# A hybrid decoder layer on one core: second score product on 128 rows, vector work moved from POOL to DVE at the feed forward, adaLN products in pairs

## The chip, the cores and the metric

The program runs on one core of a Trainium2 chip. The metric is the device time of one execution in microseconds (us). The engines are named as in the profile: PE (TensorE, matmuls; PEld is its weight load), DVE (VectorE), ACT (ScalarE), POOL (GpSimd) and SP (SyncE, which here only issues DMAs).

## The reference, cut to what matters

One layer runs over 1024 prompt rows and 32 sample rows (1056 rows in all), D_MODEL 1024, 8 heads of 64, everything in float32:

```python
mod = silu(c) @ w_ada + b_ada
sh1, sc1, g1, sh2, sc2, g2 = split(mod, 6)
h = rmsnorm(x) * (1 + sc1) + sh1
z = h @ w_in + b_in
s = (q . k) / 8 + C_q - C_k
o = softmax(causal(s)) @ v
m = sigmoid(z_a) * (o @ w_pa) + sigmoid(z_b) * (conv_branch(z) @ w_pb + b_pb)
x = x + g1 * (m @ w_o)
h2 = rmsnorm(x) * (1 + sc2) + sh2
f_gate, f_up = split(h2 @ w_ffn_in, 2)
x = x + g2 * ((silu(f_gate) * f_up) @ w_ffn_out)
```

The conditioning vector c gives six adaLN vectors of 1024; the sixth, g2, is used only in the last line. Outputs are the normalised x and the new keys, values, forget values and convolution states.

## The kernel before, in words

The kernel keeps activations transposed (channels on the 128 partitions, rows in the free dimension). Every float32 operand of a large product is split into a high and a low float32r part, and a product is the sum of three matmuls: high by high, high by low, low by high. ACT makes the high part by a copy, DVE or POOL the low part by a subtraction.

A tile framework takes the program as written and chooses the order of each engine's instructions itself, with a planner that simulates the program with its own costs. What it may not change is the data flow and what goes through `in_order` (keep_in_program_order). `tc.high_priority(offset)` lets instructions be planned as if they had been written that much earlier. On the chip each engine, and each engine's DMA queue (SP's, ACT's, POOL's), then works strictly in the planned order, and an instruction whose semaphore is not there holds up all that stand behind it. Tiles of one tag share `bufs` buffers, so a load waits until the buffer's last reader is done.

The stages in order of time: start, first adaLN vectors and first projections (0 to 125 us); values, queries, keys, decode attention, GLU and convolution (125 to 430); prompt attention with gate projections (`gate`) and adaLN products as filler (430 to 672); remaining gates, branch products and `w_o` (672 to 895); entry of the feed forward (895 to 990); feed forward's first product (990 to 1400) and its second (1400 to 1671).

The places that the change touches:

- `ada(i, ...)`, L153: one adaLN vector. For each of 8 tiles k of `w_ada` (128x1024, 512 KB) SP loads a tile `wa` (L158), then four matmuls of 32 columns of the array run on it (L162). For vectors 2 to 5 the tile lies in the tag `wr` of pool `wp`, three buffers that are also those of the gate weights (L306) and of the feed forward's raw weights (L1117). Vectors 2 to 5 are called after the gates 6, 5, 4 and 3 in the loop over gates behind the attention; the planner moves them into the attention as filler.
- `softmax_rows(h, i, ...)`, L803: the scores of head h, block i of 128 rows, in stretches of 512 keys: L813 multiplies the tile `q` (128 rows: high and low part of the query) by `k` (the key's high part twice), L815 adds the mask on the diagonal, L816 multiplies the query's high part by the key's low part on the 64 rows `sl` only. There are 12 such stretches for each of 8 heads, 96 in all. DVE then takes the minimum (L818), ACT the exponential (L824), and `weighted` transposes (L871) and multiplies with the values (L883, L884).
- `load_head(h)`, L834: SP loads q (L846), k (L847), the 64 rows of kl (L848, 256 KB), ck (L849) and vh (L850).
- `half_factors`, L991: the factors of a Strassen-like product for half of the rows (528 columns as two times 264); L1030 and L1033 are subtractions on POOL, `split_u` (L1018) takes the low part on DVE or POOL (L1020).
- `split_w`, L302, its low part at L315; with `w_o` and the last third of the rows every second tile goes to POOL.
- `pair_weights(t, eng)`, L1128: seven weight factors from two raw tiles, with four add or subtract instructions of 128x512 (L1134, L1136, L1137, L1139) on DVE, or on POOL where a weight serves one half of the rows (t = 1, 2, 3, both times). `split` (L1120) makes the high part on ACT (L1124) and the low part on DVE (L1125); L1167 multiplies.

Of the kernel before, what the change touches and what calls it, by code (L numbers as in the profile page):

```python
# [9 lines left out]
F32 = mybir.dt.float32  # L10
# [35 lines left out]
KS = 2  # L46
NHR = 8
HF = 2
DV = (0,)
UW = KL + NP + DB * (KL + DT)  # L50


# [35 lines left out]
def hybrid_step(ctx, tc, xT, cT, vec, bvf, con, stT, ptab, ptabr, kcT, vc, lfc, w_ada, w_in, w_vfa, w_vfb,  # L88
# [64 lines left out]
    def ada(i, pl, tag, bufs, psum):  # L153

        ps = psum()
        for k in range(KD):
            w = pl.tile([P, KD, P], F32, name="wa", tag=tag, bufs=bufs).rearrange("p a b -> p (a b)")
            d = sp.dma_start(w, w_ada[k * P:(k + 1) * P, i * 1024:(i + 1) * 1024])  # L158
            if i < 2:
                in_order(d)  # L160
            for g in range(4):
                pe.matmul(ps[32 * g:32 * g + 32, :256], cTt[:, k, :], w[:, g * 256:(g + 1) * 256],  # L162
                          start=(k == 0), stop=(k == KD - 1))
        with tc.high_priority() if i < 2 else nullcontext():
            s = ev(wp, "gev", 4)
            d = act.copy(s[:, :256], ps[:, :256])
            if i == 1:
                in_order(d)
            pt = psum()
            for q in range(2):  # L170
                pe.transpose(pt[:, q * P:(q + 1) * P], s[:, q * P:(q + 1) * P], ident)
            src = pt[:, :256].rearrange("p (q g r) -> p g q r", q=2, g=4)[:, :, :, 0:9]
            b = V[:, V_ADA + i * 8:V_ADA + i * 8 + 8].rearrange("p (g q) -> p g q", g=4)
            dve.tensor_tensor(mod[:, i * 8:(i + 1) * 8, :].rearrange("p (g q) r -> p g q r", g=4),
                              src, b.unsqueeze(3).broadcast_to([P, 4, 2, 9]), OP.add)
            if i == 1:
                gains(0, V_RMS1, 8)
# [624 lines left out]

    def softmax_rows(h, i, t, ck, q, k, kl):  # L803

        sl = slice(64 * (h % 2), 64 * (h % 2) + 64)
        n = P * (i + 1)
        m = sm.tile([P, 4], F32, name="mx", tag="mx", bufs=6)
        prev = 3e38
        qb = slice(i * P, (i + 1) * P)
        for nm, s0 in enumerate(range(0, n, 512)):  # L810
            w = min(512, n - s0)
            ps = ps_s()
            pe.matmul(ps[:, :w], q[:, qb], k[:, s0:s0 + w], start=True, stop=False)  # L813
            if s0 + w == n:
                pe.matmul(ps[:, w - P:w], identr, maskr, start=False, stop=False)  # L815
            pe.matmul(ps[:, :w], q[sl, qb], kl[sl, s0:s0 + w], start=False, stop=True)  # L816

            dve.tensor_tensor_reduce(out=t[:, s0:s0 + w], in0=ps[:, :w], in1=ck[:, s0:s0 + w], scale=1.0, scalar=prev,  # L818
                                     op0=OP.add, op1=OP.min, accum_out=m[:, nm:nm + 1])
            prev = m[:, nm:nm + 1]  # L820
        cq = Cq[:, i, h:h + 1]
        st = sm.tile([P, 4], F32, name="st", tag="st", bufs=6)
        dve.scalar_tensor_tensor(st[:, 1:2], prev, cq, cq, op0=OP.subtract, op1=OP.add)
        act.activation(t[:, :n], t[:, :n], AF.Exp, bias=st[:, 1:2], scale=-1.0, accum_out=st[:, 2:3])  # L824
        dve.reciprocal(st[:, 3:4], st[:, 2:3])
        if h % 2 and i % 2:
            act.activation(t[:, :n], t[:, :n], AF.Copy, scale=st[:, 3:4])
        else:
            dve.tensor_scalar(t[:, :n], t[:, :n], st[:, 3:4], None, OP.mult)
        return t  # L830
# [3 lines left out]
    def load_head(h):  # L834

        p, h2 = divmod(h, 2)
        qd, kd = qkD[p]
        sl = slice(64 * h2, 64 * h2 + 64)

        def head_tile(name, dt=F32R):  # L840
            return atl.tile([P, NP], dt, name=name, tag=f"{name}{h2}", bufs=1)

        q, k, kl = head_tile("q2"), head_tile("k2"), head_tile("kl")
        ck, vh = head_tile("ck", F32), head_tile("vh").rearrange("p (b n) -> p b n", n=P)
        for r in range(2):
            sp.dma_start(q[64 * r:64 * r + 64, :].bitcast(F32), qd[r ^ h2][sl, :])  # L846
            sp.dma_start(k[64 * r:64 * r + 64, :].bitcast(F32), kd[0][sl, :])  # L847
        sp.dma_start(kl[sl, :].bitcast(F32), kd[1][sl, :])  # L848
        sp.dma_start(ck, cD[h:h + 1, :].broadcast_to([P, NP]))  # L849
        sp.dma_start(vh.bitcast(F32), vD[p][:, :, h2, :])  # L850
        heads[h] = (q, k, kl, ck, vh)
# [59 lines left out]
        weighted(*x)  # L911
    for i in (9, 8, 6, 5, 4, 3, 2, 1, 0):
        gate(i, pool, sp)
        if 3 <= i < 7:
            ada(8 - i, wp, "wr", 3, ps_mm)
    gains(1, V_RMS2, 32)
    atl.release()
# [75 lines left out]
    def half_factors(q, new):  # L993
# [21 lines left out]
                act.copy(u[:, :, n:], msf[:, 4 * i:4 * i + 4, :])  # L1015
            return u

        def split_u(b, k, u, eng=dve):  # L1018
            act.copy(b[0][:, k, :], u[:, k, :])
            eng.tensor_tensor(b[1][:, k, :], u[:, k, :], b[0][:, k, :].bitcast(F32), OP.subtract)  # L1020

        ks = [slice(KS * k, KS * k + KS) for k in range(4 // KS)]
        u11, u21, u12, u22 = [modulated(i, half) for half in range(2) for i in range(2)]
# [3 lines left out]
        for k in ks:  # L1027
            split_u(b21, k, u21)
        for k in ks:
            pool.tensor_tensor(u11[:, k, :], u12[:, k, :], u11[:, k, :], OP.subtract)  # L1030
            split_u(t1, k, u11)
        for k in ks:
            pool.tensor_tensor(u12[:, k, :], u22[:, k, :], u12[:, k, :], OP.subtract)  # L1033
            split_u(b22, k, u22, pool)
            dve.tensor_tensor(u22[:, k, :], u22[:, k, :], u11[:, k, :], OP.subtract)
            split_u(t2, k, u22)
        for k in ks:
            split_u(t3, k, u12, pool)
        for k in ks:
            dve.tensor_tensor(u21[:, k, :], u21[:, k, :], u22[:, k, :], OP.subtract)  # L1040
            split_u(t4, k, u21)
# [26 lines left out]
    for c in range(3):  # L1068
        o = CW3 * c
        s = sm.tile([P, 400], F32, name="s1", tag="ssum", bufs=2)  # L1070
        for j in range(KD):

            where = () if c == 0 and j < 2 else (lt2, ("wh3", "wl3"), 3)
            w = split_ahead(w_o[j], KD, pool if c == 2 and j % 2 else dve, *where)
            xr = ev(lt2, "xr", 3)
            for ch, (co, cn) in enumerate(CH):
                lo, hi = max(o, co), min(o + CW3, co + cn)
# [47 lines left out]
        dve.tensor_tensor(w[:, 1, :n], raw, w[:, 0, :n].bitcast(F32), OP.subtract)  # L1125
        return w

    def pair_weights(t, eng):  # L1128

        g, u = [raw_tile(w_fi[r * HT + t], KD * P) for r in range(2)]  # L1130
        a11, a12, a21, a22 = g[:, :512], g[:, 512:], u[:, :512], u[:, 512:]
        ws = [split(a11), split(a12)]
        s1 = ev(fb or uq, "s1", 2 if fb else 1, (P, 512))
        eng.tensor_tensor(s1, a21, a22, OP.add)  # L1134
        ws.append(split(s1))
        eng.tensor_tensor(a21, a11, a21, OP.subtract)  # L1136
        eng.tensor_tensor(a11, s1, a11, OP.subtract)  # L1137
        ws.append(split(a11))
        eng.tensor_tensor(a12, a12, a11, OP.subtract)  # L1139
        ws.append(split(a12))  # L1140
        ws.append(split(a21))
        ws.append(split(a22))
        return ws
# [7 lines left out]
    def hidden(t, halves):  # L1151


        with tc.high_priority(offset=OW if len(halves) == 2 else ON):
            w = pair_weights(t, dve if len(halves) == 2 or t in DV else pool)
        for q in halves:
            hidden_half(t, q, w)

# [40 lines left out]

    for t in range(NF):  # L1200
        hidden(t, (0,))
        if t == HF:
            B.append(half_factors(1, lambda: by_four(
                [x[:, i, :] for x in [lt.tile([P, 4, T], F32R, name="c", tag=tag, bufs=1) for tag in ("XA", "XB")] for i in range(4)] +
# [194 lines left out]
```

## Time and profile before

| | us |
|---|---|
| three runs, median (lowest to highest) | 1672.14 (1669.34 to 1674.14) |
| the profiled execution | 1673.01 |
| its span, first to last instruction | 1671.2 |
| PE busy in the span | 1600.6 |
| DVE busy | 1074.1 |
| ACT busy | 702.6 |
| POOL busy | 251.9 |

The busy time of PE is that of modelled, pipelined matmuls: a matmul's recorded duration includes its latency, so what it costs in a full queue is read from the distance between two starts. The granted clock is 1.00 at 2.4 GHz and 0.50 at 1.2 GHz.

### The profile page before, as it was taken

How to read it: one execution, taken by the hardware profiler on the slowest of the kernel's cores; microseconds unless marked ns; L12 is line 12 of the kernel's file. 1: busy time of each engine (PE TensorE's matmuls, PEld its weight loads, DVE VectorE, ACT ScalarE, POOL GpSimd, SP SyncE). 2: the span in 40 equal slices, each digit the busy share in tenths (PEclk: the TensorE clock that was granted, in tenths of full speed). 3: DMA queues.
4: the chain of work that ended last, by engine and by line, in shares of the span. 5: the costliest groups of instructions: out<-in, count | busy, mean ns of one | idle time of the engine just before them, and what ended most of it. 6: DMA issues, size and time to landing. Idle time of an engine off the chain costs nothing.

```text
span 1671.2 us, 29144 instructions
## 1 busy us (share of the span) xinstructions
PE 1600.6 (96%) x10988; PEld 1486.8 (89%) x10988; DVE 1074.1 (64%) x2119; ACT 702.6 (42%) x1395; POOL 251.9 (15%) x185
## 2 busy tenths in 40 slices
PE   6999999999999999999999789999999999999997
PEld 4999978788867777989998779999999999999997
DVE  6943389999787757234678995555555587324654
ACT  4552212122476555434554554333333365324442
POOL 2121113332220001125305430000000030000000
PEclk9999999999999979999999899999999999999998
DMA  9186576877486654354674322222222246424552
GB/s 363 62 285 185 159 226 176 249 234 224 150 247 211 185 166 145 114 187 123 211 219 156 102 85 101 77 77 77 77 82 83 80 155 214 157 87 146 172 184 84
DMA packets 143087, 263.93 MB, mean 158 GB/s; under 512 B 26810, under 2 KB 84794, under 8 KB 142306
## 3 DMA queue, kind: packets, MB, share of 16 engines
q1 hardware_dynamic: 104466, 211.46, 40.6%
q10 hardware_dynamic: 36384, 43.01, 7.4%
q0 software_dynamic: 2096, 7.60, 1.5%
q8 instruction: 86, 1.41, 0.4%
q14 instruction: 55, 0.45, 0.1%
HBM read 208.54 MB, written 53.48 MB: 157 GB/s over the span
## 4 chain that ended last, share of the span: by engine, by line
PE 70%; DVE 14%; DMA 7%; issue 3%; ACT 3%; SPq 2%; POOL 1%; ACTq 0%; DVEq 0%; POOLq 0%
PE mm L1167 23%; PE mm L1268 15%; DVE acc L525 7%; PE mm L326 6%; PE mm L324 6%; PE mm L325 6%; PE ptr L871 2%; PE pss L816 2%; DMA wa<-w_ada 1%; DMA gev<-gD 1%; PE ppv L884 1%; DVE wc L1125 1%; PE mm L162 1%; PE ppv L883 1%; PE pss L813 1%
## 5 line engine op out<-in xcount | busy, mean ns | idle before, releaser
L324 PE MATMUL mm<-ah,wh 128*128 128x384 f32 (+2 forms) x768 | 254.2, 332 | 7.4 <-ACT ah L288 3.6
L1268 PE MATMUL mm<-f,wo 128*128 128x352 f32 x1584 | 256.7, 323 | 0.0
L1268 PEld LDWEIGHTS mm<-f,wo 128*128 128x128 f32 x1584 | 254.7, 188 | 0.0
L326 PE MATMUL mm<-ah,wl 128*128 128x384 f32 (+2 forms) x768 | 253.0, 331 | 1.5 <-POOL wl L315 1.5
L325 PE MATMUL mm<-al,wh 128*128 128x384 f32 (+2 forms) x768 | 254.2, 331 | 0.0
L1167 PE MATMUL mm<-b,wc 128*128 128x264 f32 x1680 | 229.6, 288 | 10.3 <-ACT gev L1172 6.9
L1167 PE MATMUL mm<-c,wc 128*128 128x264 f32 x1776 | 235.5, 286 | 3.3 <-DVE gev L1189 3.3
L1167 PEld LDWEIGHTS mm<-c,wc 128*128 128x128 f32 x1776 | 225.2, 189 | 3.7 <-DVE gev L1189 3.7
L1167 PEld LDWEIGHTS mm<-b,wc 128*128 128x128 f32 x1680 | 217.0, 191 | 11.7 <-ACT gev L1172 7.3
L315 POOL TENSOR_TENSOR wl<-wr,wh 128x1024 fp32r<-128x1024 f32 (+1 forms) x48 | 122.1, 2547 | 440.3 <-ACT wh L312 417.3
L525 DVE SCALAR_TENSOR_TENSOR acc<-u,vec,acc 128x1024 f32<-128x1024 f32 x120 | 174.1, 1472 | 1.2
L324 PEld LDWEIGHTS mm<-ah,wh 128*128 128x128 f32 x768 | 146.5, 191 | 19.2 <-issue 7.9
L325 PEld LDWEIGHTS mm<-al,wh 128*128 128x128 f32 x768 | 146.6, 191 | 12.2 <-issue 11.7
L326 PEld LDWEIGHTS mm<-ah,wl 128*128 128x128 f32 x768 | 146.4, 191 | 7.6 <-issue 4.9
L1219 DVE TENSOR_TENSOR wo<-wr,wo 128x512 fp32r<-128x512 f32 x108 | 69.7, 647 | 129.7 <-ACT wo L1218 129.1
L1124 ACT CAST wc<-wr 128x512 fp32r<-128x512 f32 x144 | 88.0, 620 | 131.2 <-PE mm L1167 123.9
L1125 DVE TENSOR_TENSOR wc<-wr,wc 128x512 fp32r<-128x512 f32 x144 | 108.6, 760 | 37.1 <-ACT wc L1124 36.0
L1218 ACT CAST wo<-wr 128x512 fp32r<-128x512 f32 x108 | 63.2, 585 | 150.3 <-PE mm L1268 145.4
L312 ACT CAST wh<-wr 128x1024 fp32r<-128x1024 f32 (+1 forms) x72 | 68.1, 951 | 91.3 <-PE mm L325 71.9
L1134 POOL TENSOR_TENSOR s<-wr 128x512 f32<-128x512 f32 x6 | 13.1, 2188 | 400.6 <-DMA wr<-w_fi 387.1
L326 PE MATMUL mm<-yh,wl 128*128 128x352 f32 x192 | 61.9, 325 | 1.2 <-POOL wl L315 1.2
L324 PE MATMUL mm<-b,wh 128*128 128x352 f32 x192 | 62.1, 323 | 0.8 <-ACT wh L312 0.8
(299 smaller groups left out, 2731.6 us busy)
## 6 DMA issues: line engine op xcount, KB each, us to landing
wr<-w_fi SPq DMA_DIRECT2D x52, 512.0 KB
wa<-w_ada SPq DMA_DIRECT2D x48, 512.0 KB
wr<-w_fo SPq DMA_DIRECT2D x36, 512.0 KB
kt<-kcT SPq DMA_DIRECT2D x64, 256.0 KB
vt<-vc SPq DMA_DIRECT2D x64, 256.0 KB
wr<-w_o SPq DMA_DIRECT2D x24, 512.0 KB
hD<-h ACTq DMA_DIRECT2D x44, 264.0 KB
wr<-w_in SPq DMA_DIRECT2D x18, 512.0 KB
```

The source lines that it names most:

```text
L312: d = act.copy(wh[:, r, :], raw[:, r, :])
L315: eng.tensor_tensor(wl[:, r, :], raw[:, r, :], wh[:, r, :].bitcast(F32), OP.subtract)
L324: pe.matmul(ps[:, :n], wh[:, k, :], xh, start=(k == 0), stop=False)
L325: pe.matmul(ps[:, :n], wh[:, k, :], xl, start=False, stop=False)
L326: pe.matmul(ps[:, :n], wl[:, k, :], xh, start=False, stop=(k == nk - 1))
L525: dve.scalar_tensor_tensor(a[:, :NP], u[:, j:j + NP], wv[:, j:j + 1], a[:, :NP], op0=OP.mult, op1=OP.add)
L1124: act.copy(w[:, 0, :n], raw)
L1125: dve.tensor_tensor(w[:, 1, :n], raw, w[:, 0, :n].bitcast(F32), OP.subtract)
L1167: pe.matmul(ps[:, :HS], w[i][:, r, k * P:(k + 1) * P], x[s][:, k, :], start=(new and k == 0 and j == 0), stop=(k == 3 and j == 2), skip_gr ...
L1218: act.copy(x[:, 0, :], raw)
L1219: dve.tensor_tensor(x[:, 1, :], raw, x[:, 0, :].bitcast(F32), OP.subtract)
L1268: pe.matmul(ps[e][:, :n], w[r][:, k * P:(k + 1) * P], f[x], start=(k0 + k + i == 0), stop=(k0 + k == HT - 1 and i == 2))
```

## The change

`ada`: for the vectors 2 to 5 the tiles are loaded two at a time; the product of the second tile is issued first, and that of the first tile behind it is kept in program order. The vector 5 (the sixth) is no longer computed behind gate 3 but inside the feed forward, behind the first weight tile. In `load_head` all of q, k and kl are loaded on 128 rows, and L816 uses all of them (so it adds the product of the low parts). POOL's subtractions and additions in `half_factors`, `split_u`, `pair_weights` and the split of `w_o` go to DVE.

```diff
@@ ada
-        for k in range(KD):
+        def load(k):
             w = pl.tile([P, KD, P], F32, name="wa", tag=tag, bufs=bufs).rearrange("p a b -> p (a b)")
             d = sp.dma_start(w, w_ada[k * P:(k + 1) * P, i * 1024:(i + 1) * 1024])
             if i < 2:
                 in_order(d)
+            return w
+
+        def product(k, w, first, last, pinned=False):
             for g in range(4):
-                pe.matmul(ps[32 * g:32 * g + 32, :256], cTt[:, k, :], w[:, g * 256:(g + 1) * 256],
-                          start=(k == 0), stop=(k == KD - 1))
+                mm = pe.matmul(ps[32 * g:32 * g + 32, :256], cTt[:, k, :], w[:, g * 256:(g + 1) * 256],
+                               start=first, stop=last)
+                if pinned:
+                    in_order(mm)
+
+        if i < 2:
+            for k in range(KD):
+                product(k, load(k), k == 0, k == KD - 1)
+        else:
+            for k in range(0, KD, 2):
+                w0, w1 = load(k), load(k + 1)
+                product(k + 1, w1, k == 0, False)
+                product(k, w0, False, k == KD - 2, True)
@@ softmax_rows
-            pe.matmul(ps[:, :w], q[sl, qb], kl[sl, s0:s0 + w], start=False, stop=True)
+            pe.matmul(ps[:, :w], q[:, qb], kl[:, s0:s0 + w], start=False, stop=True)
@@ load_head
         for r in range(2):
-            sp.dma_start(q[64 * r:64 * r + 64, :].bitcast(F32), qd[r ^ h2][sl, :])
-            sp.dma_start(k[64 * r:64 * r + 64, :].bitcast(F32), kd[0][sl, :])
-        sp.dma_start(kl[sl, :].bitcast(F32), kd[1][sl, :])
+            rows = slice(64 * r, 64 * r + 64)
+            sp.dma_start(q[rows, :].bitcast(F32), qd[r][sl, :])
+            sp.dma_start(k[rows, :].bitcast(F32), kd[0][sl, :])
+            sp.dma_start(kl[rows, :].bitcast(F32), kd[1][sl, :])
@@ the gates behind the attention
-        if 3 <= i < 7:
+        if 4 <= i < 7:
             ada(8 - i, wp, "wr", 3, ps_mm)
@@ half_factors
         for k in ks:
-            pool.tensor_tensor(u11[:, k, :], u12[:, k, :], u11[:, k, :], OP.subtract)
+            dve.tensor_tensor(u11[:, k, :], u12[:, k, :], u11[:, k, :], OP.subtract)
             split_u(t1, k, u11)
         for k in ks:
-            pool.tensor_tensor(u12[:, k, :], u22[:, k, :], u12[:, k, :], OP.subtract)
-            split_u(b22, k, u22, pool)
+            dve.tensor_tensor(u12[:, k, :], u22[:, k, :], u12[:, k, :], OP.subtract)
+            split_u(b22, k, u22)
...
         for k in ks:
-            split_u(t3, k, u12, pool)
+            split_u(t3, k, u12)
@@ w_o
-            w = split_ahead(w_o[j], KD, pool if c == 2 and j % 2 else dve, *where)
+            w = split_ahead(w_o[j], KD, dve, *where)
@@ pair_weights (eng was dve or pool)
-        eng.tensor_tensor(s1, a21, a22, OP.add)
+        dve.tensor_tensor(s1, a21, a22, OP.add)
...
-        eng.tensor_tensor(a21, a11, a21, OP.subtract)
-        eng.tensor_tensor(a11, s1, a11, OP.subtract)
+        dve.tensor_tensor(a21, a11, a21, OP.subtract)
+        dve.tensor_tensor(a11, s1, a11, OP.subtract)
...
-        eng.tensor_tensor(a12, a12, a11, OP.subtract)
+        dve.tensor_tensor(a12, a12, a11, OP.subtract)
@@ the feed forward's first weight tiles
     for t in range(NF):
         hidden(t, (0,))
+        if t == 0:
+            ada(5, wp, "wr", 3, ps_mm)
```

## Rows read from the trace of the kernel before

**Rows 1.** Head of the page and PE's row of its part 1

```profile
span 1671.2 us, 29144 instructions
PE 1600.6 (96%) x10988; PEld 1486.8 (89%) x10988; DVE 1074.1 (64%) x2119; ACT 702.6 (42%) x1395; POOL 251.9 (15%) x185
```

**Rows 2.** Stretches: length, busy us (instructions) per engine, PE clock, DMA share, GB/s

```profile
893.00:990.00 97.00, 76.45 (x521) 73.97 (x519) 94.77 (x153) 55.47 (x117) 50.92 (x31) 0.89 0.28 89
1000.00:1340.00 340.00, 340.00 (x2787) 340.00 (x2787) 186.95 (x351) 132.01 (x284) 2.91 (x2) 1.00 0.24 82
1365.00:1386.00 21.00, 17.74 (x131) 17.32 (x130) 19.32 (x31) 12.46 (x28) 9.21 (x7) 0.92 0.46 156
435.00:650.00 215.00, 210.34 (x1328) 157.98 (x1326) 153.69 (x501) 126.73 (x262) 23.45 (x23) 0.96 0.64 189
```

**Rows 3.** PE in order of time in the attention: start, us, engine, line

```profile
495.26 0.39 PE L813 MATMUL pss<-k,q 128*128 128x512 f32 x1
495.49 0.22 PE L815 MATMUL pss<-maskr,identr 128*128 128x128 f32 x1
495.64 0.50 PE L816 MATMUL pss<-kl,q 64*128 64x512 f32 x1
496.07 0.44 PE L324 MATMUL mm<-ah,wh 128*128 128x384 f32 x1
496.35 0.34 PE L325 MATMUL mm<-al,wh 128*128 128x384 f32 x1
496.53 0.34 PE L326 MATMUL mm<-ah,wl 128*128 128x384 f32 x1
```

**Rows 4.** PE in order of time, adaLN products among the attention's

```profile
465.71 0.62 PE L162 MATMUL mm<-wa,cT 128*32 128x256 f32 x2
...
519.25 1.06 PE L162 MATMUL mm<-wa,cT 128*32 128x256 f32 x12
520.23 0.39 PE L883 MATMUL ppv<-pth,vh 128*128 128x256 f32 x1
...
531.55 0.64 PE L162 MATMUL mm<-wa,cT 128*32 128x256 f32 x8
532.12 0.38 PE L883 MATMUL ppv<-pth,vh 128*128 128x256 f32 x1
532.34 0.28 PE L884 MATMUL ppv<-ptl,vh 128*128 128x256 f32 x1
...
646.24 0.64 PE L162 MATMUL mm<-wa,cT 128*32 128x256 f32 x8
```

**Rows 5.** SP's DMA queue, its waits, 435 to 660, then 880 to 1000

```profile
SPq L158 <- PE mm L162: 51.4, 18, 16.2
...
SPq L1117 <- DVE wc L1125: 39.8, 5, 13.3
```

**Rows 6.** Order of time at 594 us, then two stretches

```profile
594.27 1.08 PE L162 MATMUL mm<-wa,cT 128*32 128x256 f32 x8 [2.63 <-DMA wa<-w_ada]
...
590.00:600.00 10.00, 7.37 (x36) 4.96 (x36) 4.86 (x17) 6.72 (x14) 2.36 (x1) 0.65 0.67 227
600.00:610.00 10.00, 10.00 (x34) 7.99 (x33) 4.00 (x19) 4.68 (x11) 0.00 (x0) 0.50 0.50 110
```

**Rows 7.** Costly groups, 893 to 990 us, then 1000 to 1340; last the chain

```profile
L1134 POOL TENSOR_TENSOR s<-wr 128x512 f32<-128x512 f32 x3 | 8.5, 2847 | 20.3 <-DVE b L1020 8.2 <-DMA wr<-w_fi 6.8 <-DVE ry L211 5.3
...
L1125 DVE TENSOR_TENSOR wc<-wr,wc 128x512 fp32r<-128x512 f32 x19 | 19.8, 1051 | 0.0
...
L1125 DVE TENSOR_TENSOR wc<-wr,wc 128x512 fp32r<-128x512 f32 x99 | 68.9, 699 | 35.3 <-ACT wc L1124 34.3
...
937.85 0.59 DVE wc L1125
```

**Rows 8.** POOL in order of time, first and last of one weight tile's four

```profile
1359.87 1.29 POOL L1134 TENSOR_TENSOR s<-wr 128x512 f32<-128x512 f32 x1 [19.88 <-DMA wr<-w_fi]
...
1363.90 1.59 POOL L1139 TENSOR_TENSOR wr<-wr 128x512 f32<-128x512 f32 x1
```

More of the change, by code (lines that the diff above doesn't have):

```diff
@@ L48 @@
 HF = 2
-DV = (0,)
 UW = KL + NP + DB * (KL + DT)
@@ L803, in softmax_rows @@
     def softmax_rows(h, i, t, ck, q, k, kl):
-        sl = slice(64 * (h % 2), 64 * (h % 2) + 64)
         n = P * (i + 1)
@@ L1016, in modulated, with split_u @@
             return u
-        def split_u(b, k, u, eng=dve):
+        def split_u(b, k, u):
             act.copy(b[0][:, k, :], u[:, k, :])
-            eng.tensor_tensor(b[1][:, k, :], u[:, k, :], b[0][:, k, :].bitcast(F32), OP.subtract)
+            dve.tensor_tensor(b[1][:, k, :], u[:, k, :], b[0][:, k, :].bitcast(F32), OP.subtract)
         ks = [slice(KS * k, KS * k + KS) for k in range(4 // KS)]
@@ L1126, in split, with pair_weights @@
         return w
-    def pair_weights(t, eng):
+    def pair_weights(t):
         g, u = [raw_tile(w_fi[r * HT + t], KD * P) for r in range(2)]
@@ L1154, in hidden @@
         with tc.high_priority(offset=OW if len(halves) == 2 else ON):
-            w = pair_weights(t, dve if len(halves) == 2 or t in DV else pool)
+            w = pair_weights(t)
         for q in halves:
```

## The prediction, before the changed kernel ran

> **What bounds the kernel now.** The page comes first: PE is busy 1600.6 of 1671.2 us, every other engine two thirds or less [rows 1]. So the question is where PE's queue loses time, and busy shares can't say that, because a matmul's recorded time includes its latency. I read the stretches next [rows 2], and in each the number of matmuls. From 1000 to 1340 us PE does 2787 matmuls in 340 us, 0.122 us each at a granted clock of 1.00: that stage is PE's own pace and the change leaves it alone. Three stretches fall short. At the feed forward's entry (893 to 990) it does 521 in 97 us. About 105 of these are `w_o`'s with 352 columns at some 0.16 us (0.122 times 352/264), the rest at 0.122: an estimate of 67 us of work in 97, with the clock at 0.89. From 1365 to 1386 it does 131 where 172 would fit (21/0.122), so 5 us are lost. And in the attention (435 to 650) it is "busy" 210.3 of 215 us, yet the distances of starts in PE's order of time [rows 3] show a queue that moves in jerks. At the entry DVE is the engine that never rests, 94.8 of 97 us [rows 2]; in the attention it is PE, with DVE at 153.7 and ACT at 126.7 of 215.
>
> **Second score product on all rows.** In [rows 3] a 512-column matmul (L813) lets the next start after 0.23 us. The L815 behind it, 128 columns, should take a quarter of that, 0.06, and takes 0.15; L816, 512 columns on 64 rows, takes 0.43; the L324 after it 0.28, while L325, of the same 384 columns, takes 0.18. So 0.09 are lost before the 64-row product, 0.20 in it and 0.10 behind it, 0.39 us in all; the only thing special there is that the number of array rows changes from 128 to 64 and back. With 128 rows throughout these go, and the added rows cost nothing as far as these rows show, since a matmul's pace follows its columns. 96 products times 0.39 are 37 us, all on PE's queue, which sets this stage. I don't take all of it: the rest of a score's way (DVE's minimum, ACT's exponential, the loads of the next head) doesn't get faster, and 37 us out of 215 leave PE 178 for DVE's 154 and ACT's 127. I take four fifths, **-30 us**; the ends are -37 (nothing else becomes late) and -10 (the loads set the pace, second rival).
>
> The Trainium skill (TensorEngine Tiling (Array Packing), Key Properties) says that changing the tiling mode drains the engine; the rows above agree in kind. By TensorE: Matmul & The Clock Gate (Single matmul latency; Back-to-back issue gap) an isolated 512-column matmul takes (398+512)/2.4 = 379 ns where a streamed one takes 216; as an estimate, two drains of 163 ns for 96 products are 31 us, and with four fifths the term would be -25 instead of -30.
>
> **The low keys on both halves.** One more DMA of 256 KB per head on SP, eight in all, 2 MB, at the 227 GB/s of [rows 6] about 1.1 us each; no engine but SP issues them. They are covered as long as the head loads come in time, and eight loads of 512 KB leave this stage with the sixth vector. 0 us; without cover at most 9.
>
> **adaLN products by twos.** A product (four matmuls, eight records, side by side in the array's columns) that stands alone moves PE's queue on by 0.57 us, and the matmul behind it by 0.22 where 0.12 are due (256/512 of 0.23) [rows 4]. A run of twelve records takes 0.98, so a second product in the same run costs about 0.41. Standing alone thus costs 0.16, plus 0.10 behind, plus before it about the 0.09 of [rows 3]: 0.35 us. The 32 products now stand in 37 separate runs (first and last in [rows 4]; some are cut in pieces). In pairs there would be 16: 21 times 0.35, 7 us, if no pair is cut. The second half of each is pinned, the first isn't, so I take **-5 us** (ends 0 and -7). The price is a wait: the first product now needs the second tile. Behind it on PE stand the next scores, transposes and value products. On SP the next adaLN load waits until a buffer is free: already 51.4 us in 18 waits, the longest 16.2 [rows 5], with the next head's loads behind it in that queue. A pair takes two of the three buffers, so those waits get longer. How often PE pays the trace can't say; one such stall stands in it and is priced in the third rival. I keep one, as now, and count 0; the ends are -11 (it goes) and +22 (two more).
>
> **The sixth vector inside the feed forward.** Its 8 products leave the attention, 8 times 0.57, 5 us, and come back as four pairs of about 0.98 plus 0.2 each, 5 us, at a place where PE waits for DVE anyway. But its eight loads use the same three buffers as the raw weights, whose loads already wait 39.8 us for DVE to free one [rows 5]: four pairs of 1 MB, 4.6 us each at the 227 GB/s of [rows 6], hold two buffers for some 20 us, if nothing hides them. Together I take **+4 us** (ends -5 and +20). Its result is needed only by the second product, after 1400 us.
>
> **POOL's work to DVE at the entry.** What moves, with its count from the program: 16 instructions of 128x528 and 12 of 128x512, at 0.60 us of DVE each (two DVE splits of that size start so far apart [rows 7]), and two of `w_o`'s splits at 1.2: 19 us more on an engine that is busy 94.8 of 97. What it gains: DVE's split L1125 takes 1051 ns here and 699 where POOL rests [rows 7], half again as long. If all of DVE's work here were stretched so, it would take 94.8/1.5 = 63 us alone, and 82 with the moved work, 13 less than now. Instructions that read PSUM and the small ones may be stretched less, so I take **-8 us**. The ends are +19 (nothing is stretched by POOL) and -26: PE's own 67 us are the floor, and four pairs of the sixth vector fit in.
>
> **POOL's work to DVE at 1365 us.** One tile's four instructions take POOL 5.6 us, from 1359.87 to 1365.49 [rows 8], where DVE needs 2.4; the split and PE wait behind them. Two such tiles would give 6; lost are 5 in all. **-4 us**, ends 0 and -5.
>
> **The sum.** -30 -5 +4 -8 -4 = -43 us, against the profiled execution's own 1673.0 us (span 1671.2, and 1.8 around it; 0.9 over the median of the runs). That is **1630 us**.
>
> **The rivals.** *First: DVE is freed by all that POOL held.* If every microsecond of POOL's 50.9 at the entry [rows 2] had cost DVE one, DVE would need 94.8-50.9+19 = 63 us, PE's 67 would set the entry, and the term is -26: **1612 us**. For it: POOL's instruction itself takes 2847 ns where its like take 1290 [rows 7, 8], so both sides suffer. Against: L1125 shows a half, not a doubling. The Trainium skill (SBUF — State Buffer, SBUF: two separate sides) states that the shared ports are an exclusive lock for the whole instruction, which would make this the case; the L1125 rows above bear it out in part only.
>
> *Second: the attention is set by its loads.* The DMA engines are busy 0.64 of those 215 us [rows 2], 138 us of full work, in bursts at the head loads; PE's time to spare is before the bursts, not in them. Then the score term is -10 and the rest stays: **1650 us**. For it: SP's waits. Against: PE's lost time is spread over all 96 products, not gathered at the loads.
>
> *Third, slower: pairs starve PE.* At 594 us PE idles 2.6 us for one tile of `w_ada`, and the clock is then 0.65 and 0.50 of full (1.2 GHz) for two stretches of 10 us [rows 6], which costs 3.5+5.0 more: 11 us a stall. Sixteen pairs each wait for two tiles through three buffers. From four such stalls more on, the 43 us are gone; with five it is 1630+55 = **1685 us**. Against: there is one such stall in 37 runs now, and the planner puts the first product behind both loads. The Trainium skill (TensorE: Matmul & The Clock Gate, Why this matters for your kernels) warns of just this loop with a DMA wait between bursts; one place of this trace agrees.
>
> *Fourth: the change does not do what it says*, if the jerks come from writing one PSUM bank in turn rather than from the row count. Then only the other terms are left: -5 +4 -8 -4, **1660 us**. Against: L815 follows L813 into the same bank with no gap [rows 3].
>
> **How the numbers follow.** Forecast 0.56, first rival 0.17, second 0.17, third 0.06, fourth 0.04. The range leaves out the third rival, part of the fourth and the low corner where every term is at its best (-37 -7 -11 -5 -26 -5, 1582): **1598 to 1658 us**. 0.3% is 5 us, about what a measurement of this kernel can tell from no change. Faster by more than that are all cases but the third and a tail of the fourth, 0.91; within it 0.04; slower 0.05.
>
> **What would show it.** Behind L813 and L815 the distance of starts at L816 should be 0.23 for 512 columns and the attention some 30 us shorter; adaLN products in about 16 runs; at the entry L1125 near 700 ns, POOL all but empty, DVE still the busiest, the stretch near 90 us; no loss at the second place. The forecast is wrong if PE's gaps in the attention turn into waits for DMAs or ACT as large as what the switches gave back, if the entry gets longer because SP's weight loads stand behind the sixth vector's, or if the clock drops more often than now.

## The result, and the profile after

| | before | after |
|---|---|---|
| median (lowest to highest), us, same chip | 1672.95 (1669.34 to 1674.14) | 1643.20 (1640.61 to 1645.14) |
| the profiled execution | 1673.01 | 1640.61 |
| its span | 1671.2 | 1638.8 |

The ratio is 0.9825, 95% interval 0.9803 to 0.9847: 29 us faster. Forecast were 43 us, 1630 us with a range of 1598 to 1658. Direction and range held; a third of the gain is missing.

The head of the page of the kernel after:

```profile
span 1638.8 us, 29126 instructions
...
PE 1558.8 (95%) x10988; PEld 1478.3 (90%) x10988; DVE 1060.2 (65%) x2163; ACT 701.4 (43%) x1395; POOL 177.9 (11%) x141
```

POOL's time fell by 74 us, and PE is still the engine that is always busy. As before [rows 1], that says nothing about where PE's queue loses time. The stretches do; these are the windows of the kernel after that answer to [rows 2], moved to where the same work now lies:

```profile
856.00:953.00 97.00, 75.27 (x528) 68.33 (x528) 80.69 (x176) 54.07 (x112) 0.10 (x1) 0.88 0.38 128
970.00:1300.00 330.00, 330.00 (x2708) 330.00 (x2707) 180.73 (x342) 128.08 (x276) 0.00 (x0) 1.00 0.23 82
1332.00:1353.00 21.00, 19.16 (x153) 18.52 (x152) 20.25 (x42) 14.74 (x34) 0.00 (x0) 1.00 0.54 182
435.00:630.00 195.00, 181.43 (x1330) 160.78 (x1329) 161.79 (x523) 134.71 (x279) 26.74 (x23) 0.97 0.68 197
```

The second stretch is PE's own pace as before (330 us for 2708 matmuls, 0.122 each). The attention now does 1330 matmuls in 195 us where 1328 took 215. The entry does 528 in 97, against 521, but 64 of the 528 are records of the sixth vector's products (8 products of 8 records each): 464 are left for the entry's own work, less than before, although DVE now rests 16 of the 97 us and POOL does nothing. The reason is in the order of time at the entry.

PE in order of time at the entry, adaLN products (L162 is now L165, L1167 is L1182):

```profile
885.77 1.94 PE L165 MATMUL mm<-wa,cT 128*32 128x256 f32 x16 [5.34 <-DMA wa<-w_ada]
...
893.20 1.07 PE L165 MATMUL mm<-wa,cT 128*32 128x256 f32 x16
...
897.58 1.07 PE L165 MATMUL mm<-wa,cT 128*32 128x256 f32 x16 [1.00 <-DMA wa<-w_ada]
903.73 1.93 PE L165 MATMUL mm<-wa,cT 128*32 128x256 f32 x16 [5.08 <-DMA wa<-w_ada]
```

Windows of the same place:

```profile
880.00:890.00 10.00, 4.66 (x32) 3.26 (x33) 6.65 (x15) 4.07 (x7) 0.00 (x0) 0.66 0.44 116
890.00:900.00 10.00, 7.65 (x78) 6.11 (x77) 6.83 (x33) 2.40 (x7) 0.10 (x1) 1.00 0.78 277
900.00:910.00 10.00, 6.28 (x36) 4.77 (x37) 7.94 (x20) 6.22 (x15) 0.00 (x0) 0.66 0.58 215
910.00:920.00 10.00, 5.96 (x26) 4.83 (x24) 9.86 (x17) 10.00 (x24) 0.00 (x0) 0.66 0.00 0
```

Three of the sixth vector's four pairs keep PE waiting for their loads, 11.4 us together, and in three of the four stretches of 10 us around them the granted clock is 0.66 on average, so for a part of each it is at its lower level, 1.2 GHz. The first and the last pair run there: 1.94 and 1.93 us against 1.07 for the others.

The score products, PE in order of time, the kernel after (compare [rows 3]; L813, L815, L816 are L827, L829, L830):

```profile
482.42 0.41 PE L827 MATMUL pss<-k,q 128*128 128x512 f32 x1
482.67 0.22 PE L829 MATMUL pss<-maskr,identr 128*128 128x128 f32 x1
482.73 0.45 PE L830 MATMUL pss<-kl,q 128*128 128x512 f32 x1
483.01 0.28 PE L899 MATMUL ppv<-ptl,vh 128*128 128x256 f32 x1
```

The mask product moves the queue on by 0.06 us instead of 0.15, the second score product by 0.28 (the median of 47 such is 0.23) instead of 0.43. At 512 columns the jerks are gone.

**Where PE's time went.** For each matmul take the distance to the next start, take off the idle time that the trace puts ahead of the next, and the time due for its columns at full clock (0.232 us for 512, 0.122 for 264, as in undisturbed stretches). What is left is loss, put down to its place; matmuls that start at half clock have a line of their own. For the attention, from the first score product to the first branch product, in us:

| | before | rows alone | pairs alone | rows + DVE | after, sixth back | after |
|---|---|---|---|---|---|---|
| length | 293.7 | 276.0 | 292.9 | 270.3 | 271.0 | 263.3 |
| due time | 215.2 | 215.2 | 215.2 | 215.2 | 212.0 | 211.7 |
| ahead of, in and behind the second score product | 34.6 | 8.8 | 35.6 | 8.6 | 8.8 | 8.0 |
| around adaLN products | 16.0 | 14.1 | 11.9 | 14.0 | 6.8 | 5.8 |
| PE waits | 4.7 | 18.2 | 6.1 | 12.9 | 20.2 | 17.5 |
| half clock | 9.9 | 5.9 | 10.3 | 5.2 | 8.6 | 5.8 |
| other | 13.3 | 13.8 | 13.8 | 14.4 | 14.6 | 14.5 |

(Rows alone, pairs alone and "after, sixth back" are the first, second and fourth run of the next section, rows + DVE the first of its last part. "After, sixth back" does 24 matmuls of the gates, 3.4 us, ahead of this stage; with them its length is 274.4.)

Each column is one execution, and executions differ: the profiled one of the kernel after has the lowest of its four times, that of rows alone the highest of its four. By how much the attention can differ, four kernels show: after, sixth behind tile 5, sixth behind tile 9 and sixth spread have all 1752 matmuls of the attention in the same order (and DVE's and POOL's instructions and SP's loads too), and its length is 263.3, 270.3, 270.4 and 270.4. So a difference of some us between two columns, of the waits above all, can't be put down to a change of the kernel by itself.

And for the feed forward's first product, from its first to its last matmul (weight tiles counted from 0):

| | before | DVE alone | after, sixth back | after | behind tile 5 | behind tile 9 | spread |
|---|---|---|---|---|---|---|---|
| length | 499.5 | 485.6 | 485.4 | 503.7 | 503.5 | 501.0 | 494.5 |
| due time without adaLN | 462.4 | 462.4 | 462.4 | 462.5 | 462.5 | 462.5 | 462.5 |
| adaLN products | 0 | 0 | 0 | 4.3 | 4.1 | 4.4 | 8.4 |
| PE waits for `wa` | 0 | 0 | 0 | 11.4 | 8.4 | 6.8 | 0 |
| PE waits for ACT or DVE | 24.0 | 12.8 | 11.7 | 12.0 | 14.9 | 14.6 | 13.4 |
| half clock | 7.9 | 6.4 | 7.0 | 9.3 | 8.5 | 7.1 | 5.5 |
| other | 5.2 | 4.0 | 4.3 | 4.2 | 5.1 | 5.6 | 4.7 |

### The profile page after: what moved, and what is told of

Same layout as the page of the kernel before. It is cut to its first block, busy times and chain, and to the rows that moved or that the text cites. A ratio compares the mean times of both kernels' runs of the same rounds, so it can differ in the third digit from the quotient of the medians.

```text
span 1638.8 us, 29126 instructions
## 1 busy us (share of the span) xinstructions
PE 1558.8 (95%) x10988; PEld 1478.3 (90%) x10988; DVE 1060.2 (65%) x2163; ACT 701.4 (43%) x1395; POOL 177.9 (11%) x141
## 3 DMA queue, kind: packets, MB, share of 16 engines
q8 instruction: 86, 1.41, 0.3%
## 4 chain that ended last, share of the span: by engine, by line
PE 71%; DVE 14%; DMA 7%; issue 2%; ACT 2%; POOL 2%; SPq 0%; ACTq 0%; DVEq 0%; POOLq 0%
PE mm L1182 25%; PE mm L1285 16%; DVE acc L540 7%; PE mm L341 7%; PE mm L339 7%; PE mm L340 7%; DMA wa<-w_ada 3%; PE ptr L886 1%; POOL wl L330 1%; PE mm L573 1%; PE mm L572 1%; PE mm L165 1%; PE mm L574 1%; PE ppv L899 1%; DMA wr<-w_fi 1%
## 5 line engine op out<-in xcount | busy, mean ns | idle before, releaser
L1182 PE MATMUL mm<-b,wc 128*128 128x264 f32 x1680 | 232.3, 289 | 8.4 <-ACT wc L1139 4.9
L1182 PE MATMUL mm<-c,wc 128*128 128x264 f32 x1776 | 235.0, 285 | 1.8 <-ACT gev L1187 1.4
L1182 PEld LDWEIGHTS mm<-b,wc 128*128 128x128 f32 x1680 | 218.5, 192 | 11.9 <-ACT wc L1139 6.5
L1182 PEld LDWEIGHTS mm<-c,wc 128*128 128x128 f32 x1776 | 223.9, 188 | 2.7 <-ACT gev L1187 2.0
L340 PEld LDWEIGHTS mm<-al,wh 128*128 128x128 f32 x768 | 145.3, 189 | 11.5 <-issue 10.4
L330 POOL TENSOR_TENSOR wl<-wr,wh 128x1024 fp32r<-128x1024 f32 (+1 forms) x44 | 111.3, 2532 | 387.5 <-ACT wh L327 337.6
L1140 DVE TENSOR_TENSOR wc<-wr,wc 128x512 fp32r<-128x512 f32 x144 | 98.1, 689 | 36.3 <-ACT wc L1139 35.4
L1187 ACT COPY gev<-mm 128x264 f32<-128x264 f32 x132 | 49.1, 376 | 32.6 <-PE mm L1182 29.9
```

The lines of the kernel that those rows point to most:

```text
L330: eng.tensor_tensor(wl[:, r, :], raw[:, r, :], wh[:, r, :].bitcast(F32), OP.subtract)
L340: pe.matmul(ps[:, :n], wh[:, k, :], xl, start=False, stop=False)
L1182: pe.matmul(ps[:, :HS], w[i][:, r, k * P:(k + 1) * P], x[s][:, k, :], start=(new and k == 0 and j == 0), stop=(k == 3 and j == 2), skip_gr ...
```

## The experiments

Every ratio is against the kernel before on the same chip, and us are that ratio times 1670. Line numbers of diffs are left out; `+`/`-` are against the kernel named.

**One part at a time.** Three kernels each make one part of the change on the kernel before; their edits are the hunks of the diff ahead of the prediction. The fourth is the kernel after with the sixth vector where it was:

```diff
@@ after, the gates behind the attention
-        if 4 <= i < 7:
+        if 3 <= i < 7:
             ada(8 - i, wp, "wr", 3, ps_mm)
@@ after, feed forward
-        if t == 0:
-            ada(5, wp, "wr", 3, ps_mm)
```

Hunks `softmax_rows` and `load_head` alone (this adds low by low to the scores, as the change does):

> The kernel before with the second score product on 128 rows alone (and the low keys loaded on both halves). Theory (the change of array rows cost 0.39 us a product, PE sets the attention, four fifths are kept): 25 to 32 us less than before, L813 to L815 to L816 at 0.23, 0.06 and 0.23 us. Rival (the attention is set by its loads, and the pairs or the moved sixth vector brought the gain): about 10 us less.

Measured: 1646.85 us, ratio 0.9877 (0.9847 to 0.9908), -20.5 us: between the theory's 25 to 32 and the rival's 10, so neither holds as stated.

Hunk `ada` alone, for the vectors 2 to 5, the sixth behind gate 3 as before:

> The kernel before with the adaLN products in pairs alone, the sixth vector still behind gate 3. Theory (what the fewer switches give, the waits for the second tile take back): between 4 us less and 4 us more than before. Rival (the pairs bring their 7 us): 5 to 8 us less. A second rival (pairs starve PE): 10 us more or worse.

Measured: 1667.25 us, ratio 0.9998 (0.9983 to 1.0014), 0 us, as the theory said.

The hunks that move POOL's work to DVE, alone:

> The kernel before with POOL's work at the feed forward on DVE alone, no sixth vector there. Theory (the gain is real, and the sixth vector's loads ate it in the changed kernel): 10 to 16 us less than before, the entry shorter by 8 to 11, nothing lost at the second place. Rival (DVE is full either way, so the moved work costs what POOL's rest gives): 0 to 4 us less, from the second place alone.

Measured: 1650.78 us, ratio 0.9907 (0.9876 to 0.9938), -15.5 us: the theory held in time and at the entry; at the second place 2.8 of the 5 us stayed lost (149 matmuls in 21 us where 172 would fit).

The kernel after with the sixth vector back:

> The changed kernel with the sixth vector back behind gate 3 (in pairs). Theory (its loads hold up PE and the weights at the entry, 11 us of waits and the half clock behind them): 5 to 10 us less than the changed kernel's 1643, the entry some 12 us shorter and the attention 4 us longer. Rival (the entry is set by DVE, the sixth vector hides in PE's waits): 3 to 6 us more than the changed kernel.

Measured: 1628.60 us, ratio 0.977 (0.9743 to 0.9797), -38.4 us. That is some 9 us faster than the kernel after, as the theory said, whose interval (0.9803 to 0.9847) lies wholly above.

*What follows.* The three parts add up to -36, what the fourth kernel has; the sixth vector inside the feed forward costs these 9 us (0.9825 less 0.977, times 1670; by the two intervals roughly 3 to 15). The waits of PE in the attention (columns: what waits, total us, times, longest) show where the gain of the score product is lost. Before, then rows alone:

```profile
PE mm L162 <- DMA wa<-w_ada: 3.3, 2, 2.6
PE ppv L884 <- DVE ptl L874: 0.8, 1, 0.8
```

```profile
PE ptr L871 <- DVE ptl L874: 7.4, 4, 3.8
PE mm L162 <- DMA wa<-w_ada: 5.8, 5, 3.0
PE pst L777 <- DVE lnsum L775: 1.6, 1, 1.6
PE pss L812 <- DVE mx L817: 1.4, 2, 1.0
PE pss L815 <- DMA kl<-qkD: 0.9, 1, 0.9
```

By the table the places around the product give back 25.8 us, the half clock 4.0, the adaLN products' surroundings 1.9; new waits take 13.5. DVE's steps of the softmax are late in most of these, some 9 us more than before; the adaLN loads in 2.5 us more, the low keys' loads in one wait of 0.9.

The entry of the kernel with DVE alone, waits of PE from 880 to 985 us:

```profile
PE mm L1167 <- ACT wc L1124: 5.0, 3, 3.1
PE mm L1167 <- DVE wc L1125: 4.8, 3, 2.3
PE mm L1167 <- ACT b L1124: 0.7, 1, 0.7
```

The window that answers to the entry of [rows 2], and the costliest group of DVE there, 888 to 985 us:

```profile
888.00:985.00 97.00, 86.47 (x612) 84.52 (x611) 91.77 (x200) 61.63 (x127) 0.10 (x1) 0.91 0.33 105
```

```profile
L1125 DVE TENSOR_TENSOR wc<-wr,wc 128x512 fp32r<-128x512 f32 x22 | 14.7, 692 | 0.0
```

PE does 612 matmuls here instead of 521, and DVE 200 instructions in 91.8 us instead of 153 in 94.8. The split takes 692 ns, where its mean was 1051 with POOL at work and 699 where POOL rested [rows 7]. PE's waits for ACT and DVE in this stage fall from 24.0 to 12.8 us.

The 1051 is a mean of two kinds. Of those 19 splits 13 take 0.68 to 0.69 us, and six take 1.41 to 2.46, each beside a running POOL instruction. DVE and POOL in order of time, the kernel before:

```profile
967.62 0.68 DVE L1125 TENSOR_TENSOR wc<-wr,wc 128x512 fp32r<-128x512 f32 x1
...
974.69 1.48 POOL L1033 TENSOR_TENSOR u<-u 128x528 f32<-128x528 f32 x1
974.94 1.78 DVE L1125 TENSOR_TENSOR b<-wr,b 128x512 fp32r<-128x512 f32 x1
976.13 1.76 POOL L1020 TENSOR_TENSOR c<-u,c 128x528 fp32r<-128x528 f32 x1
976.64 1.80 DVE L1125 TENSOR_TENSOR wc<-wr,wc 128x512 fp32r<-128x512 f32 x1
```

Against the medians of the same instructions in the kernel with DVE alone, 28 of DVE's instructions in the entry's 97 us took longer, by 1.1 us in the median whether they last 0.16 us alone or 0.7: 29 us together. As many ran beside POOL without loss.

**Is it the change of row count?** The kernel before, with the 64-row product cut in two of half the columns, side by side in the same bank:

```diff
-            pe.matmul(ps[:, :w], q[sl, qb], kl[sl, s0:s0 + w], start=False, stop=True)
+            for a in (0, w // 2):
+                pe.matmul(ps[:, a:a + w // 2], q[sl, qb], kl[sl, s0 + a:s0 + a + w // 2], start=False, stop=a > 0)
```

> The kernel before with each second score product on 64 rows cut in two of half the columns, so 192 in place of 96, two behind one another. Theory (what costs is the change of the number of rows, once in and once out): the second of the two follows the first at the pace of its columns, 256 columns in about 0.12 us, and the time is that of before within 4 us. Rival (each 64-row matmul, or each further write to the same PSUM bank, costs its 0.3 us or more): 25 to 40 us more than before.

Measured: 1667.82 us, ratio 0.9987 (0.9963 to 1.0011), no difference, as the theory said; the rival's 25 to 40 us more are out. PE in order of time:

```profile
497.41 0.39 PE L813 MATMUL pss<-k,q 128*128 128x512 f32 x1
497.73 0.50 PE L817 MATMUL pss<-kl,q 64*128 64x256 f32 x2
498.16 0.44 PE L324 MATMUL mm<-ah,wh 128*128 128x384 f32 x1
498.44 0.22 PE L813 MATMUL pss<-k,q 128*128 128x128 f32 x1
```

L813 moves on by 0.32 instead of 0.23, the two narrow products by 0.43 together, the L324 behind by 0.28: exactly the one wide product of [rows 3]. So the 0.20 is not paid for each 64-row product. Nor does it grow with the columns: in the kernel before the distance behind L816 is 0.254 us at 128 columns, 0.311 at 256, 0.369 at 384 and 0.428 at 512 (medians of 14 to 46), a constant 0.20 on top of 0.06 for each 128. The 0.09 ahead and the 0.10 behind are the same from 256 to 512 columns too (medians of 11 to 46); at 128 the one ahead is 0.14. It is a price of the change of rows. What the engine does in that time (a drain, or a weight load that can't be hidden) these runs do not tell.

**Where can the sixth vector go?** Three kernels put it elsewhere in the feed forward. Behind weight tile 5 instead of tile 0, then behind tile 9 (counted from 0; `NF` is 4 and `NK` 2, and each line stands in the loop over its tiles):

```diff
@@ after, feed forward, e5
-        if t == 0:
+        if t == NF + 1:
             ada(5, wp, "wr", 3, ps_mm)
@@ e6
+        if t == NF + NK + 3:
```

> The changed kernel with the sixth vector behind weight tile 5 instead of tile 0, where each weight tile serves both halves of the rows and PE has 20 us of work from one. Theory (what it cost at tile 0 are waits for its loads in a stretch without spare work for PE): it costs no more there than its own 5 us, and the kernel comes out 3 to 6 us below the one with the sixth vector back behind gate 3, that is 41 to 45 us below the kernel before. Rival (the three buffers are short wherever it stands): as slow as the changed kernel, 29 us below before.

Measured: 1645.15 us, ratio 0.9853 (0.983 to 0.9875), -24.5 us.

> The same with the sixth vector still later, behind weight tile 9, after the raw weights have got a fourth buffer. Theory: 41 to 45 us below before, the same as behind tile 5. Rival (the fourth buffer is what counts): 3 us or more better than behind tile 5.

Measured: 1644.69 us, ratio 0.9854 (0.9827 to 0.9881), -24.4 us.

*What follows.* My theory that a place where PE has no other waits would hide the loads fell, and the fourth buffer of the raw weights, which the second of the two has, changed nothing (the loads of `w_ada` have three in both). Waits of PE, tile 5, 970 to 1010 us:

```profile
PE mm L165 <- DMA wa<-w_ada: 8.4, 3, 3.4
```

The window of that place:

```profile
990.00:1000.00 10.00, 5.66 (x40) 2.98 (x41) 1.29 (x2) 1.41 (x3) 0.00 (x0) 0.52 0.62 215
```

Waits of PE, tile 9, 970 to 1100 us:

```profile
PE mm L165 <- DMA wa<-w_ada: 6.8, 2, 3.5
```

Eight loads in a row through three buffers keep PE waiting at each of the three places tried, and where PE was at its own pace the whole wait is lost time.

Then the loads of the vectors 2 to 5 were taken off SP's queue, on top of the kernel with tile 5:

```diff
-            d = sp.dma_start(w, w_ada[k * P:(k + 1) * P, i * 1024:(i + 1) * 1024])
+            d = (sp if i < 2 else pool).dma_start(w, w_ada[k * P:(k + 1) * P, i * 1024:(i + 1) * 1024])
```

> The kernel with the sixth vector behind tile 5, and the loads of vectors 2 to 5 issued by POOL's queue instead of SP's. Theory (the pairs' waits in the attention come from loads that stand in SP's queue behind the next head's loads): PE's waits for adaLN tiles in the attention fall from 10 us to under 4, the time by 5 to 10 us against the same kernel with SP's queue. Rival (they come from the buffers and from full DMA engines): no change within 3 us.

Measured: 1662.77 us, ratio 0.9964 (0.9942 to 0.9985), -6 us: 18 worse than the same kernel with SP. A miss; in the attention PE waits as long for these loads as with SP (13.6 there), and for one thing more. Waits of PE, 409 to 690 us:

```profile
PE mm L339 <- ACT yh L956: 9.2, 1, 9.2
PE mm L165 <- DMA wa<-w_ada: 12.3, 6, 2.8
```

The attention is 280.5 us long against 270.3; that is all of the 10.1 us by which the two profiled executions differ, the other 8 of the 18 stand in no trace. Which instruction of POOL or ACT was held up, and how, I did not follow up.

**Pairs or singles, bunched or spread.** Rows and DVE on the kernel before, with single adaLN products and the sixth behind gate 3; then the kernel after with the sixth vector spread out, a load written ahead of a weight tile and its product behind it, one tile at a time from tile 6 on; then the same with single products for the vectors 2 to 4:

```diff
@@ spread: after, feed forward
+    sixth = ada_steps(5)
...
+        next(sixth, None)
...
+        next(sixth, None)
@@ ada_steps: one step loads, the next multiplies
+            w = wp.tile([P, KD, P], F32, name="wa", tag="wr", bufs=3).rearrange("p a b -> p (a b)")
+            sp.dma_start(w, w_ada[k * P:(k + 1) * P, i * 1024:(i + 1) * 1024])
+            yield
+            for g in range(4):
+                pe.matmul(ps[32 * g:32 * g + 32, :256], cTt[:, k, :], w[:, g * 256:(g + 1) * 256],
+                          start=(k == 0), stop=(k == KD - 1))
...
+            yield
```

> The kernel before with two parts alone: the score product on all rows and the entry's POOL work on DVE; the adaLN products stay single and the sixth vector stays behind the gate of the third group. Theory (the parts add up and the pairs bring nothing): -20.5 and -15.5 add to -36, about 1633 us against 1669, and the kernel with the pairs as well (measured at -38) is no better than this by more than 2. Rival (the pairs only pay once the attention is shorter, since PE has less slack to lose): this run gives no more than -30, and the pairs are worth 8 or more in that kernel.

Measured: 1634.01 us, ratio 0.9779 (0.9729 to 0.9829), -36.9 us. The theory held: the parts add, and the kernel with pairs is no better than this by more than 2. The interval is wide, though (-28 to -45): what pairs are worth on top is known to within some 9 us only, and the rival's -30 lies inside it.

> The kernel after, with the sixth adaLN vector spread over the feed forward: from the seventh weight tile on, one load of w_ada is written ahead of a tile and its product behind it, so that 20 us of PE work lie between a load's start and its use. Theory (what the sixth vector cost at the entry, and behind the fifth and the ninth tile, was PE's wait for its loads, three buffers for eight loads in a row): no wait of PE for wa in the feed forward, the entry's loss back at 20 us; the time is that of the sixth vector behind the third gate (-38) less the 3 to 5 us that its products take in the attention: -41 to -44. Rival (the products in the feed forward disturb it by themselves, through the clock or the weight loads' queue, however they are fed): -25 to -30, as in the two late places.

Measured: 1639.15 us, ratio 0.9818 (0.9772 to 0.9863), -30.4 us. Half a miss. PE has no wait for `wa` in the feed forward, as the theory said, and the entry is as good as without the sixth vector; but the time is the rival's. PE in order of time, the first piece of one such product (the runs of L1200 are cut by the view's window):

```profile
1020.68 0.90 PE L1200 MATMUL mm<-c,wc 128*128 128x264 f32 x6
1021.50 0.62 PE L206 MATMUL ppv<-wa,cT 128*32 128x256 f32 x2
1022.05 1.14 PE L1200 MATMUL mm<-c,wc 128*128 128x264 f32 x7
```

Two of its eight records take 0.55 us, and a whole product in one run takes 0.57; 0.09 are lost ahead of each run and 0.11 in the matmul behind it. The planner cut three of the eight products in two, so there are 11 runs of about 0.76, the 8.4 us of the table. Where PE never waits all of that is paid. In return the attention is 4 us shorter in the traces (274.4, with the 3.4 us done ahead of it, to 270.4).

> As the spread kernel, but with the vectors two to four as single products between the score and value products, as in the kernel before. Theory (pairs bring nothing in the attention, they only bunch the loads): within 2 us of the spread kernel with pairs, or 1 to 3 better since PE's waits for wa in the attention (10 us in the kernel after) fall towards 3. Rival (pairs halve the runs and each run costs): 3 to 6 us slower than with pairs.

Measured: 1642.31 us, ratio 0.9839 (0.9793 to 0.9886), -26.9 us, 3.5 behind the kernel with pairs, the intervals overlapping almost wholly. PE waits for `wa` in the attention fell to 5.2 us, but one wait of 5.9 for ACT stands at its end. This does not tell the two apart.

## Why the prediction was right, and where it was wrong

**Second score product: -30 forecast, -20.5 alone.** The mechanism is the one forecast: at 512 columns all of [rows 3]'s three losses vanish. The term was mis-sized in its gross, "96 products times 0.39 are 37 us": over the attention the places around the product held 34.6 us and gave back 25.8, 0.27 a product. The 0.39 was read at one product of 512 columns; half of the 96 are narrower and keep a loss of some 0.05 us in them (0.229 from start to start at 384 columns in the median, where a plain product of 384 takes 0.18 [rows 3]). The share kept, "four fifths", came out nearly: 20.5 of 25.8 by the runs, 17.7 by the traces. The reason given holds too: PE waits 13.5 us more, against which 5.9 less stand at half clock and around adaLN products. The second rival had the right kind of event, but the loads are only a quarter of the new waits; most are DVE's. Its end, -10, was not reached either. The fourth rival (writing one bank in turn) is out: the first and the second score product still write the same bank, and the losses are gone.

The prediction's estimate for two drains, each an isolated matmul's latency less a streamed one's, was 31 us by the Trainium skill (TensorEngine Tiling (Array Packing), Key Properties; TensorE: Matmul & The Clock Gate, Single matmul latency). The places around the product held 34.6 us before and gave back 25.8, so the trace agrees in size.

**Low keys on both halves: 0.** Right: one wait of 0.9 us for `kl` in the rows-alone kernel.

**adaLN products by twos: -5 forecast, 0 measured (-2.8 to +2.3).** The saving is there, but smaller: around adaLN products 16.0 falls to 11.9 alone, 4.1 of the 7 us. The prediction's condition "if no pair is cut" failed: 25 runs are left, not 16, since the planner cut pairs in pieces. The rest went back in small items that one trace can't tell from chance (PE's waits for `wa` are 3.8 us there, 3.3 before). In the shorter attention of the full change the step that failed is "I keep one [stall], as now, and count 0". On top of rows and DVE (rows + DVE against after, sixth back) the pairs leave 21 runs of 34, save 7.2 around the products and pay 7.3 in waits and 3.4 at half clock. Waits of PE for `wa` there, singles, then pairs:

```profile
PE mm L162 <- DMA wa<-w_ada: 4.9, 4, 1.8
```

```profile
PE mm L165 <- DMA wa<-w_ada: 14.9, 8, 3.7
```

That is the third rival's mechanism, at about 1.9 us of wait and no 11 a stall (2.9 with all of the half clock), just large enough to cancel the part, not to turn the sign of the whole.

**Sixth vector inside the feed forward: +4 forecast, about +9 measured.** The step that failed is the size taken for the loads' effect, about 4 us, close to none between ends of 0 and 20: "four pairs ... hold two buffers for some 20 us, if nothing hides them". Little hides them: 11.4 us of waits, 4.3 of products and 2.3 more at half clock, 18.3 us in the feed forward with the rest. The other half of the term, the attention's relief, was forecast at 5: it is 4.0 (274.4 to 270.4) in the three traces where the sixth vector goes behind tile 5, behind tile 9 or is spread, and 11 in that of the kernel after. The order of the instructions in those four attentions is the same, so the 7 us between them are not a gain of the kernel after; they lie in how long PE waited (17.5 us against 20.8 behind tile 5) and ran at half clock (5.8 against 10.0). What made that execution shorter is open.

The Trainium skill (TensorE: Matmul & The Clock Gate, Why this matters for your kernels) warns that waits for DMAs between bursts cost the clock as well; the windows from 880 to 890 and from 900 to 920 us, at 0.66 with waits of 5.3 and 5.1 us in them or just ahead, agree.

**POOL's work to DVE: -8 and -4 forecast, together -15.5 measured (-20.7 to -10.4).** Right in kind and nearly in size. By the profile the feed forward's first product is 13.9 us shorter with this part alone, some 11 of them at the entry (91 more matmuls in its 97 us, at 0.122 each). L1125 is at 692 ns, as forecast "near 700". What the prediction read from 1051 against 699 ns, "half again as long" for all of DVE's work, is not what happens: an instruction of DVE that meets POOL's either loses some 1.1 us, whatever its size, or nothing. That this comes to 29 us in sum, near the 32 that the half gave (94.8 less 63), is luck. The -4 at the second place came to about -2.7: 153 matmuls in 21 us instead of 131, 172 due, so of 5 us lost 2.3 are left, 1.9 of them in waits for ACT. In the kernel after, the entry's share can't be seen, because the sixth vector's waits fill the room it made; the check "the stretch near 90 us" failed for that reason.

The first rival's -26 did not come: POOL did not cost DVE all of its 50.9 us but 29. By the Trainium skill (SBUF — State Buffer, SBUF: two separate sides) one engine holds the shared ports for a whole instruction and the other waits. The trace agrees better than the prediction thought: 0.68 us or, mostly, about 1.8. What was wrong in the rival is the price, since POOL's 50.9 us hold its own waits for DVE ([rows 7, 8]: 2847 against 1290 ns).

**The sum.** -20.5 + 0 + 9 - 15.5 = -27, within the interval of the 29 measured (26 to 33). Of the 16 us between the 43 forecast and these 27, 9.5 are the score term, 5 the pairs and 5 the sixth vector; POOL's part gave 3.5 more than forecast. With the sixth vector left behind gate 3 the change gives 38 us, with or without pairs.

## What to carry to other kernels

A place where the bounding engine pauses anyway does not yet hide filler work whose loads come in a bunch: the same eight products cost some 4 us among the attention's switches and 18 at the feed forward's entry, bunched, or 9 in the feed forward (by the table's lengths), spread with every load in time. When a fixed price per instruction is removed from the bounding engine, read it at several places before it is multiplied: 0.39 at one place became 0.27 over 96, and 5 to 8 of those 26 us came back, most of them as waits on the engine next in line. A mean duration can hide two kinds; look at the single instructions before it is used as a factor. And a saving that makes an instruction wait for two loads in place of one has to be weighed against those waits; here they took all of it.

## What the runs showed that was not expected

- The switch of row count from 128 to 64 and back costs 0.39 us in three places, 0.09 ahead (0.14 at 128 columns), 0.20 in and 0.10 behind, whatever the columns otherwise (128 to 512) and for one 64-row product or two.
- DVE's loss to POOL goes by the instruction met and not by size: in the entry's 97 us 28 instructions of DVE lost 1.1 us each in the median, 29 us in all, and the rest nothing.
- Eight loads of 512 KB through three buffers kept PE waiting 6.8 to 11.4 us at each of three places of the feed forward, two of them in the stage where the DMA engines are otherwise busy 0.23 of the time (970 to 1300 us of the kernel after). Spread one by one they kept it waiting nowhere.
- A run of adaLN products costs by the run: 0.55 us for a quarter of a product, 0.57 for a whole one.
- The attention lasted 263.3 us in one execution and 270.3 to 270.4 in three others with the same instructions in the same order. Whether a fourth buffer for the adaLN loads would help it was not tried.
